# Attention scores as two fp32r passes over stacked key parts, the residual parked in HBM, and the attention half of the output projection woven in by tile

## The chip, the cores and the metric

The kernel runs on one core of a Trainium2 chip. A core has five engines that run beside each other and wait for one another by semaphores: TensorE (PE, matrix products and transposes; PEld is its weight load), VectorE (DVE), ScalarE (ACT), GpSimd (POOL) and SyncE (SP, which here only issues DMA transfers). Each engine works through its own list of instructions in order. The metric is the time of one execution on the device in microseconds (us), as the median of several runs.

## The reference, cut to what matters

One decoder layer on 512 rows of 1024 numbers, all in float32: a SwiGLU block, LN1, two mixers side by side on the same rows, LN2, a second SwiGLU block with an embedding, LN3.

```python
x = layer_norm(alpha * x + 0.5 * swiglu_ffn(x, ffn1_w13[i], ffn1_w2[i]), ln1_g[i], ln1_b[i])
h = x @ w_in[i]
...
y_a = gdn_mixer(gq, gk, gv, gz, ga, gb, ...)        # gated delta rule, 4 heads of 128
y_b = diff_attention_mixer(dq, dk, dv, ...)         # below
mix = jnp.concatenate([y_a, y_b], axis=-1)
x = layer_norm(alpha * x + mix @ w_out[i], ln2_g[i], ln2_b[i])
```

The change is in the attention, whose four heads hold two maps of 64 dimensions each; their scores are `q k^T` for each map, masked, through two softmaxes, and the second map is subtracted:

```python
s = jnp.einsum("bqhmd,bkhmd->bhmqk", qb, k).astype(f32) * scale      # d = 64, m = 0, 1
s = jnp.where(qp[:, None] >= pos[None, :], s, -jnp.inf)
pr = jax.nn.softmax(s, axis=-1)
attn = pr[:, :, 0] - lam * pr[:, :, 1]
return jnp.einsum("bhqk,bkhd->bqhd", attn.astype(v.dtype), v)
```

## The kernel before

The 512 rows are four tiles `t` of 128. A weight product in near-float32 precision is made of three products in fp32r, a reduced form of float32: each operand is split in a high part (a copy rounded to fp32r, on ACT) and a low part (the operand less its high part, on DVE), and `mm3` (lines 295 to 299) multiplies high by high, low by high and high by low. `split` (line 158) makes the parts. `XH`, `XL` hold the parts of the layer's rows, transposed; `RES` is the residual, four tiles of 128 x 1024 float32 that stay in the core's memory (SBUF).

The mixers (`mix_zone`) run in one zone of SBUF, with the residual beside it. First come straight parts: the values (`values_and_gates`), the keys and queries of the delta rule (`keys_queries`). LN1 of the four tiles is still under way when they begin: `norm_natural` of each tile takes statistics on DVE (L309), a power on POOL (L314), scales on DVE (L320, L329) and on ACT and POOL (L324, L325, L326), and `norm_turn` (L341) transposes it into `XH`, `XL`. The rest is written as generators, "lanes", that yield an estimated cost and wait; `weave` interleaves them by a running clock. The lanes are the delta rule's dense part (`gdn`), its block inverse (`diagonal`), its chain over four chunks (`chain`), sixteen `attention(t, h)` lanes, `fill` (attention keys and queries, other projections), and last `out_attn` and `out_gdn`, the two halves of the output projection with the residual addition and LN2. A scheduler below this settles the final list of each engine, and may set an instruction ahead of others that were written earlier.

In `fill`, the queries and keys of one tile are transposed and copied (L1003) to `DQT` and `DKT`. An attention lane makes, for each map `m`, one float32 product of 64 rows (the map's dimensions) into PSUM tag `c` (L1156) and adds the mask by a bf16 product of 128 rows (L1157). Then follow the maximum, the exponentials, a normalising combination (L1158 to L1165), the transposes (L1169), the product with the values `DV` (L1175) and an RMS norm that puts its output back over `DQT` (L1183). `TT`, a tile of 128 x 2048, holds the delta rule's inverse blocks; it is cleared at line 851 and later takes LN2's gains.

`out_attn` opens when all sixteen heads are done. It transposes and splits the attention's output of all four tiles (`to_mix`, PSUM tag `c`, L871), takes four weights, and then makes the 96 products of `project_out`, which lie between the steps of `chain`. These are the lines of the scores:

```python
for m in range(2):
    r = slice(m * DQK, (m + 1) * DQK)
    pe.matmul(sc[m], DQT[r, h, t * P:(t + 1) * P], DKT[r, h, 0:n], start=True, stop=False)
    pe.matmul(sc[m][:, n - P:n], idb, negb, start=False, stop=True)
    dve.tensor_reduce(mx[:, m:m + 1], sc[m], AX.X, ALU.max)
```

Here `n` is the number of keys that tile `t` may see, 128 x (t + 1).

## Time and profile before

| | |
|---|---|
| median of 3 runs | 1092.85 us (1091.51 to 1092.94) |
| the profiled execution | 1093.08 us, of which the span from first to last instruction is 1091.3 us |
| mean granted TensorE clock | 0.998 of full speed |
| TensorE products busy | 1067.6 us, 98% of the span |
| VectorE, ScalarE, GpSimd busy | 76%, 45%, 10% |
| mixers, from the values to LN2 | about 355 to 684 us of the span |

A busy TensorE in the records is not TensorE at its peak: products are pipelined and their records overlap. What a product costs is read from the distance between the starts of two neighbours in the timeline, and this distance is called its pitch here.

### The profile page before, as it was taken

The numbers are of one execution on the slowest core, as the hardware profiler recorded it, in microseconds if no ns is written. First come the engines' busy times: TensorE is split into PE (matmuls) and PEld (weight loads), VectorE is DVE, ScalarE is ACT, GpSimd is POOL, SyncE is SP. The second block draws the span as 40 slices with busy tenths as digits, with TensorE's granted clock in tenths as the row PEclk, the third lists the DMA queues.
The fourth block names the chain that finished last, engine by engine and source line by source line (L and its number), as shares of the span: only waits on it lengthen the run. The fifth ranks groups of instructions, "written<-read, shape, count | busy, mean of one in ns | idle before, by whom it ended". The sixth has DMA issues, their size and how long they took to land.

```text
span 1091.3 us, 17360 instructions
## 1 busy us (share of the span) xinstructions
PE 1067.6 (98%) x6627; PEld 941.4 (86%) x6627; DVE 826.3 (76%) x1446; ACT 491.3 (45%) x950; POOL 110.9 (10%) x175
## 2 busy tenths in 40 slices
PE   9999999999999989999999999999999999999996
PEld 7889898989897968778865887789899998999895
DVE  5989796979678366357674658889988796979568
ACT  5745352535333256324365633545444453535231
POOL 1100000000002302432112203100000000000003
PEclk9999999999999999999999999999999999999999
DMA  8634332333242042124120211524342332333212
GB/s 296 200 112 117 97 114 80 117 104 110 77 127 87 1 136 78 35 73 116 40 59 1 77 36 51 177 67 142 111 123 90 110 104 88 118 105 98 78 39 97
DMA packets 44275, 106.03 MB, mean 97 GB/s; under 512 B 10848, under 2 KB 12528, under 8 KB 44192
## 3 DMA queue, kind: packets, MB, share of 16 engines
q1 hardware_dynamic: 37968, 96.71, 29.1%
q0 software_dynamic: 1808, 6.04, 1.6%
q10 hardware_dynamic: 4416, 2.16, 0.7%
q8 instruction: 52, 0.85, 0.3%
q14 instruction: 31, 0.25, 0.1%
HBM read 102.41 MB, written 2.49 MB: 96 GB/s over the span
## 4 chain that ended last, share of the span: by engine, by line
PE 55%; DVE 5%; DMA 3%; ACT 2%; POOL 2%; issue 1%; DVEq 0%; SPq 0%; ACTq 0%; POOLq 0%
PE pb L297 9%; PE pb L298 9%; PE pb L299 9%; PE pc L299 4%; PE pc L298 4%; PE pc L297 4%; PE pa L299 3%; PE pa L298 3%; PE pa L297 3%; DMA raw<-in_wa_dram 3%; PE pc L1156 2%; DVE wl L160 1%; ACT wh L159 1%; PE pa L1089 1%; PE pc L1175 1%
## 5 line engine op out<-in xcount | busy, mean ns | idle before, releaser
L160 DVE TENSOR_TENSOR wl<-raw,wh 128x1024 fp32r<-128x1024 f32 (+3 forms) x137 | 142.2, 1044 | 42.0 <-ACT wh L159 40.9
L159 ACT CAST wh<-raw 128x1024 fp32r<-128x1024 f32 (+3 forms) x137 | 122.9, 905 | 104.3 <-PE pa L298 30.7
L297 PE MATMUL pb<-wh,hh 128*128 128x512 f32 (+1 forms) x356 | 138.3, 389 | 3.5 <-DVE RES L807 1.7
L298 PE MATMUL pb<-wl,hh 128*128 128x512 f32 (+1 forms) x356 | 138.0, 388 | 0.0
L299 PE MATMUL pb<-wh,hl 128*128 128x512 f32 (+1 forms) x356 | 137.8, 387 | 0.0
L229 ACT CAST th<-tr 128x512 fp32r<-128x512 f32 x160 | 98.5, 619 | 84.5 <-PE pc L298 49.6
L233 DVE TENSOR_TENSOR tl<-tr,th 128x512 fp32r<-128x512 f32 x160 | 109.1, 684 | 11.1 <-ACT th L229 10.2
L190 ACT CAST wh<-raw 128x512 fp32r<-128x512 f32 x88 | 54.4, 622 | 133.0 <-PE pb L299 91.4
L297 PE MATMUL pb<-wh,XH 128*128 128x512 f32 (+2 forms) x288 | 110.8, 385 | 3.1 <-ACT AB L928 1.3
L298 PE MATMUL pb<-wl,XH 128*128 128x512 f32 (+2 forms) x288 | 106.7, 371 | 1.2 <-DVE wl L160 1.1
L299 PE MATMUL pb<-wh,XL 128*128 128x512 f32 (+2 forms) x288 | 106.1, 368 | 0.0
L298 PE MATMUL pa<-XL,wh 128*128 128x256 f32 (+1 forms) x344 | 100.0, 291 | 0.3 <-DVE XL L160 0.3
L299 PE MATMUL pa<-XH,wl 128*128 128x256 f32 (+1 forms) x344 | 99.9, 290 | 0.0
L297 PE MATMUL pa<-XH,wh 128*128 128x256 f32 (+1 forms) x344 | 99.9, 290 | 0.0
L297 PE MATMUL pc<-XH,th 128*128 128x256 f32 x320 | 90.6, 283 | 0.0
L298 PE MATMUL pc<-XL,th 128*128 128x256 f32 x320 | 90.6, 283 | 0.0
L299 PE MATMUL pc<-XH,tl 128*128 128x256 f32 x320 | 90.6, 283 | 0.0
L490 DVE TENSOR_TENSOR RES<-RES,pb 128x512 f32<-128x512 f32 (+1 forms) x81 | 54.6, 677 | 45.3 <-PE pb L299 44.4
L191 DVE TENSOR_TENSOR wl<-raw,wh 128x512 fp32r<-128x512 f32 x88 | 60.0, 688 | 31.2 <-ACT wh L190 30.8
L297 PEld LDWEIGHTS pb<-wh,hh 128*128 128x128 f32 x356 | 66.9, 188 | 19.1 <-DVE RES L807 2.0
L299 PEld LDWEIGHTS pb<-wh,hl 128*128 128x128 f32 x356 | 66.9, 188 | 13.6
L298 PEld LDWEIGHTS pb<-wl,hh 128*128 128x128 f32 x356 | 66.9, 188 | 13.3 <-DVE wl L191 0.3
(303 smaller groups left out, 2639.1 us busy)
## 6 DMA issues: line engine op xcount, KB each, us to landing
raw<-in_wa_dram SPq DMA_DIRECT2D x127, 512.0 KB, 3.7
raw<-in_wb_dram SPq DMA_DIRECT2D x88, 256.0 KB, 2.7
raw<-in_wd_dram SPq DMA_DIRECT2D x4, 520.0 KB, 3.6
RES<-in_xn_dram POOLq DMA_DIRECT2D x4, 512.0 KB, 6.0
gb<-in_gb_dram POOLq DMA_DIRECT2D x8, 256.0 KB, 3.9
xr<-in_xT_dram ACTq DMA_DIRECT2D x7, 256.0 KB, 4.5
out_dram<-RES SPq DMA_DIRECT2D x5, 256.0 KB, 2.1
TT<-in_gb_dram POOLq DMA_DIRECT2D x4, 256.0 KB, 3.5
```

Of the source, the lines that this page charges most:

```text
L159: return (self.nc.scalar.copy(hi, src), self.nc.vector.tensor_tensor(lo, src, hi.bitcast(F32), ALU.subtract))
L160: self.nc.vector.tensor_tensor(lo, src, hi.bitcast(F32), ALU.subtract))
L190: nc.scalar.copy(hi, r)
L191: nc.vector.tensor_tensor(lo, r, hi.bitcast(F32), ALU.subtract)
L229: act.copy(h, t)
L233: dve.tensor_tensor(hl[1], t, hl[0].bitcast(F32), ALU.subtract)
L297: pe.matmul(o, wh, xh, start=first, stop=False)
L298: pe.matmul(o, wh, xl, start=False, stop=False)
L299: pe.matmul(o, wl, xh, start=False, stop=last)
L490: dve.tensor_tensor(rj, rj, pd, ALU.add)
L1089: pe.matmul(pt[:, h * P:(h + 1) * P], MP[:, 0, c, h, :], TT[:, c, h, :], start=True, stop=True)
L1156: pe.matmul(sc[m], DQT[r, h, t * P:(t + 1) * P], DKT[r, h, 0:n], start=True, stop=False)
```

## The change

1. **Scores.** For each map the 64 rows of keys become 128: `KK[:, m]` holds the keys' high parts on the map's own rows and their low parts on the other map's rows. `QZ` holds for each head and map the query's high part on both halves (`q = m`), and the query's low part on the map's rows over zeros (`q = 2 + m`). A score is two fp32r products of 128 rows. The parts are made by ACT copies and DVE subtractions: in `fill` for the keys, and at the start of each attention lane for the queries (a new yield follows them).
2. **Residual.** The four tiles of `RES` become one tile `RESA`. After LN1 all four are stored to `XR` in HBM. The first two then serve as `TT` (cleared in `keys_queries` now, not at the zone's start), the last two as `DQT`. They are loaded again from `XR` in `out_attn`.
3. **Output projection.** `out_attn` opens when the delta rule's dense part and the gate projection are done, and takes one tile at a time, when that tile's four heads are done; `to_mix` there uses PSUM tag `b`. LN2's gains lie in `DV`. `project_out` yields half its cost after every second weight.

```diff
-        self.RES = [cp.tile([P, D], F32, name=f"RES{t}") for t in range(NT)]
+        self.RESA = cp.tile([P, NT, D], F32, name="RESA")
+        self.RES = [self.RESA[:, t] for t in range(NT)]
...
-        TT = mp.tile([P, NC, H, P], F32, name="TT")
...
-        DKT = mp.tile([P, H, S], F32, name="DKT")
-        DQT = mp.tile([P, H, S], F32, name="DQT")
+        KK = mp.tile([P, 2, H, S], F32R, name="KK")
+        QZ = mp.tile([P, 4, 4, P], F32R, name="QZ")
+        DQT = [self.RESA[:, 2 + t // 2, (t % 2) * 512:(t % 2) * 512 + 512].rearrange("p (h b) -> p h b", b=P)
+               for t in range(NT)]
+        TT = self.RESA[:, 0:2].rearrange("p c (d h b) -> p (c d) h b", d=2, b=P)
...
-        pool.memset(TT, 0.0)
+        XR = dp.tile([NT, P, D], F32, name="XR")
...
                     held = (i, h)
+                    if i == 0 and h == 2:
+                        for t in range(NT):
+                            nc.sync.dma_start(XR[t], RES[t])
+                    if i == 1 and h == 0:
+                        pool.memset(TT, 0.0)
...
-                    dve.tensor_copy((DKT if word == "k" else DQT)[:, :, t * P:(t + 1) * P], v4(pt))
+                    if word == "k":
+                        for m in range(2):
+                            r, o = rows(m), rows(1 - m)
+                            hi = KK[r, m, :, t * P:(t + 1) * P]
+                            act.copy(hi, v4(pt)[r])
+                            dve.tensor_tensor(KK[o, m, :, t * P:(t + 1) * P], v4(pt)[r], hi.bitcast(F32), ALU.subtract)
+                    else:
+                        dve.tensor_copy(DQT[t], v4(pt))
...
             n = (t + 1) * P
+            i = (t * H + h) % 4
+            qz = QZ[:, i]
+            for m in range(2):
+                r, o = rows(m), rows(1 - m)
+                act.copy(qz[r, m], DQT[t][r, h])
+                act.copy(qz[o, m], DQT[t][r, h])
+                dve.tensor_tensor(qz[r, 2 + m], DQT[t][r, h], qz[r, m].bitcast(F32), ALU.subtract)
+            yield 0, 1.5
...
-                r = slice(m * DQK, (m + 1) * DQK)
-                pe.matmul(sc[m], DQT[r, h, t * P:(t + 1) * P], DKT[r, h, 0:n], start=True, stop=False)
+                for q in (m, 2 + m):
+                    pe.matmul(sc[m], qz[:, q], KK[:, m, h, 0:n], start=q == m, stop=False)
                 pe.matmul(sc[m][:, n - P:n], idb, negb, start=False, stop=True)
...
-            yield 0.2 + 0.43 * (t + 1), 4.5 + 0.8 * t
+            yield 0.1 + 0.24 * (t + 1), 4.5 + 0.8 * t
...
-                yield 2.6, 0
+                    if k % 2:
+                        yield 1.3, 0
...
+        done = [{("attn", t, h) for h in range(H)} for t in range(NT)]
+
         def out_attn():
-            for t in range(NT):
-                to_mix(DQT[:, :, t * P:(t + 1) * P], t, 4, "c")
-                yield 0.5, 0
+            for t in (0, 1):
+                nc.sync.dma_start(RES[t], XR[t])
             w = [self.take() for _ in range(4)]
             for t in range(NT):
+                while not done[t] <= said:
+                    yield 0, 0.5
+                to_mix(DQT[t], t, 4, "b")
+                if t % 2:
+                    nc.sync.dma_start(RES[2 + t // 2], XR[2 + t // 2])
+                yield 0.5, 1.0
                 yield from project_out(w, 0, t)
...
-            gbt = [TT[:, j].rearrange("p a b -> p (a b)") for j in range(4)]
+            gbt = [DV[:, j].rearrange("p a b -> p (a b)") for j in range(4)]
...
-        need_out = {("attn",) + th for th in heads} | {"z"}
+        need_out = {("gdn", c) for c in range(NC)} | {"z"}
```

Three places in the lists of the engines show what moved. The first is TensorE's list at the first two attention heads (tile 0, 128 keys, both maps). `pc` is the PSUM tile of the scores, `wh` and `XH` are parts of a weight product that lies between. Before:

```order
L1156 MATMUL pc_5135<-DKT,DQT 128x128
L1157 LDWEIGHTS idb
L1157 MATMUL pc_5135<-LVM,idb 128x128
L1156 MATMUL pc_5152<-DKT,DQT 128x128
L1157 LDWEIGHTS idb
L1157 MATMUL pc_5152<-LVM,idb 128x128
L297 MATMUL pb_5177<-wh_4720,XH 128x512
```

And now (the lines are shifted by the edit: L1156 is L1187, L1157 is L1188, L297 is L298):

```order
L1187 MATMUL pc_5180<-KK,QZ 128x128 x2
L1188 LDWEIGHTS idb
L1188 MATMUL pc_5180<-LVM,idb 128x128
L1187 MATMUL pc_5199<-KK,QZ 128x128 x2
L1188 LDWEIGHTS idb
L1188 MATMUL pc_5199<-LVM,idb 128x128
```

One float32 product of 64 rows has become two fp32r products of 128 rows, and the mask's product behind each pair has stayed.

The second place is POOL's list around LN1 of the last two tiles (t = 2 and t = 3), where `bnrs` holds a tile's statistics. Before, the clearing of `TT` stood behind the last tile:

```order
L325 TENSOR_TENSOR RES_70<-RES_70,gb_3794 128x256
L326 TENSOR_TENSOR RES_70<-RES_70,gb_3795 128x256
L314 TENSOR_TENSOR bnrs_3979<-bnrs_3979,mhalf 128x1
L316 TENSOR_SCALAR bnrs_3979<-bnmv_3977,bnrs_3979 128x1
L325 TENSOR_TENSOR RES_71<-RES_71,gb_3794 128x256
L326 TENSOR_TENSOR RES_71<-RES_71,gb_3795 128x256
L314 TENSOR_TENSOR bnrs_4037<-bnrs_4037,mhalf 128x1
L316 TENSOR_SCALAR bnrs_4037<-bnmv_4035,bnrs_4037 128x1
L325 TENSOR_TENSOR RES_72<-RES_72,gb_3794 128x256
L326 TENSOR_TENSOR RES_72<-RES_72,gb_3795 128x256
L851 MEMSET TT 128x2048
```

Now (L314 is L315, L316 is L317, L326 is L327) it stands between tile 1 and tile 2:

```order
L326 TENSOR_TENSOR RESA<-RESA,gb_3791 128x256
L327 TENSOR_TENSOR RESA<-RESA,gb_3792 128x256
L986 MEMSET RESA 128x2048
L315 TENSOR_TENSOR bnrs_3976<-bnrs_3976,mhalf 128x1
L317 TENSOR_SCALAR bnrs_3976<-bnmv_3974,bnrs_3976 128x1
L326 TENSOR_TENSOR RESA<-RESA,gb_3791 128x256
L327 TENSOR_TENSOR RESA<-RESA,gb_3792 128x256
L315 TENSOR_TENSOR bnrs_4034<-bnrs_4034,mhalf 128x1
L317 TENSOR_SCALAR bnrs_4034<-bnmv_4032,bnrs_4034 128x1
```

The clearing has moved ahead of six operations of LN1, and it now writes over the first two residual tiles, which the stores to `XR` read.

The third place is TensorE's list where the last tile of the attention enters the output projection. Before, the last of four transposes to `XH`, `XL` stood ahead of the products of tile 0, which read other columns:

```order
L871 MATMUL pc_6337<-CST,DQT 128x128 x4
L1202 MATMUL pa_6344<-ST_4066,KQ 128x128 x2
L1210 MATMUL pa_6354<-ST_4066,KQ 128x128 x4
L871 MATMUL pc_6363<-CST,DQT 128x128 x4
L297 MATMUL pb_6370<-wh_5957,XH 128x512
L298 MATMUL pb_6370<-wl_5958,XH 128x512
L299 MATMUL pb_6370<-wh_5957,XL 128x512
```

Now the transposes of tile 3 stand directly ahead of the products of tile 3 (L874 was L871):

```order
L299 MATMUL pb_6731<-wl_6203,XH 128x512
L300 MATMUL pb_6731<-wh_6202,XL 128x512
L874 MATMUL pb_6745<-CST,RESA 128x128 x4
L298 MATMUL pb_6753<-wh_5900,XH 128x512
L299 MATMUL pb_6753<-wl_5901,XH 128x512
L300 MATMUL pb_6753<-wh_5900,XL 128x512
```

The first product behind the transposes reads what ACT makes of them, and the third what DVE makes of that.

## Rows read from the trace of the kernel before

**Rows 1.** The profile's page: span, and busy time of TensorE.

```profile
span 1091.3 us, 17360 instructions
PE 1067.6 (98%) x6627; PEld 941.4 (86%) x6627; DVE 826.3 (76%) x1446; ACT 491.3 (45%) x950; POOL 110.9 (10%) x175
```

**Rows 2.** Windows view, attention's stretch: from:to, length, then busy us of each engine.

```profile
480.00:611.00 131.00, 129.41 (x723) 97.83 (x722) 85.55 (x226) 69.75 (x158) 24.94 (x54) 1.00 0.17 50
```

**Rows 3.** Timeline of PE, two score runs: start us, duration us, instruction.

```profile
489.03 0.27 PE L1169 MATMUL pc<-CST,tt 128*128 128x128 f32 x1
489.23 0.48 PE L1156 MATMUL pc<-DKT,DQT 64*128 64x128 f32 x2
...
490.00 0.40 PE L298 MATMUL pb<-wl,XH 128*128 128x512 f32 x1
...
577.34 0.49 PE L1169 MATMUL pc<-CST,tt 128*128 128x128 f32 x3
577.75 1.12 PE L1156 MATMUL pc<-DKT,DQT 64*128 64x512 f32 x2
578.81 0.23 PE L1157 MATMUL pc<-LVM,idb 128*128 128x128 bf16 x1
578.85 0.48 PE L298 MATMUL pb<-wl,XH 128*128 128x512 f32 x1
579.16 0.40 PE L299 MATMUL pb<-wh,XL 128*128 128x512 f32 x1
```

**Rows 4.** Timeline of PE, fp32r products of 256 and of 512 columns.

```profile
360.56 0.28 PE L297 MATMUL pb<-wh,XH 128*128 128x256 f32 x1
360.68 0.28 PE L298 MATMUL pb<-wl,XH 128*128 128x256 f32 x1
...
498.00 0.40 PE L297 MATMUL pb<-XH,wh 128*128 128x512 f32 x1
498.24 0.39 PE L298 MATMUL pb<-XL,wh 128*128 128x512 f32 x1
```

**Rows 5.** Source view of line 1156: count, duration ns min/median/max, first and last start, forms.

```profile
L1156 PE MATMUL pc<-DKT,DQT x64: 272/481/693, 480.4 to 599.3; 64*128 64x128 f32 x16, 64*128 64x256 f32 x16, 64*128 64x384 f32 x16, 64*128 64x512 f32 x16
```

**Rows 6.** Groups by line and form, ACT and DVE, 380 to 612: busy us, mean ns.

```profile
L1171 ACT COPY tt<-pc 128x128 f32<-128x128 f32 x4 | 1.0, 262 | 2.0 <-PE pc L1169 2.0
L1165 DVE SCALAR_TENSOR_TENSOR tt<-pc,arr,tt 128x128 f32<-128x128 f32 x4 | 1.4, 346 | 0.0
```

**Rows 7.** Timelines of POOL, DVE, ACT and PE at LN1; brackets: idle before, releaser.

```profile
352.07 0.73 POOL L326 TENSOR_TENSOR RES<-RES,gb 128x256 f32<-128x256 f32 x1
354.60 0.99 POOL L314 TENSOR_TENSOR bnrs<-bnrs,mhalf 128x1 f32<-128x1 f32 x1 [1.80 <-DVE bnrs L313]
357.30 0.67 DVE L490 TENSOR_TENSOR RES<-RES,pb 128x512 f32<-128x512 f32 x1
363.89 1.81 POOL L851 MEMSET TT<- 128x2048 f32 x1
363.87 0.37 ACT L926 COPY DV<-pb 128x256 f32<-128x256 f32 x1 [1.02 <-POOL RES L326]
364.36 0.39 PE L297 MATMUL pb<-wh,XH 128*128 128x264 f32 x1 [1.27 <-ACT AB L928]
```

**Rows 8.** The page's DMA issues: queue, count, KB each, median us from issue to landing.

```profile
raw<-in_wa_dram SPq DMA_DIRECT2D x127, 512.0 KB, 3.7
out_dram<-RES SPq DMA_DIRECT2D x5, 256.0 KB, 2.1
```

**Rows 9.** Timeline of PE, the chain's last transposes to XH, XL and what follows.

```profile
658.15 1.02 PE L871 MATMUL pa<-CST,ta 128*128 128x128 f32 x4 [0.21 <-DVE ta L1249]
659.44 0.50 PE L297 MATMUL pb<-wh,XH 128*128 128x512 f32 x1 [0.27 <-DVE RES L1274]
```

**Rows 10.** Timeline of PE, last Gram product of the delta rule, first product with the inverse.

```profile
471.29 1.46 PE L1071 MATMUL pa<-KQ 128*128 128x256 f32 x6
503.47 0.60 PE L1089 MATMUL pa<-TT,MP 128*128 128x128 f32 x4
```

More of the change, by code (lines that the diff above doesn't have):

```diff
@@ L993, in keys_queries, with rows @@
                 pool.tensor_tensor(NRM[:, c], q1[:, c], phalf[:, 0:H], ALU.pow)
+        def rows(m):
+            return slice(m * DQK, (m + 1) * DQK)
         def fill():
@@ L1011, in fill @@
                             turn(*held)
+                    if word == "q" and t == 0:
+                        for m in range(2):
+                            pool.memset(QZ[rows(1 - m), :, 2 + m].bitcast(F32), 0.0)
                     d = tb()
@@ L1145, in attention @@
             n = (t + 1) * P
+            i = (t * H + h) % 4
+            qz = QZ[:, i]
+            for m in range(2):
+                r, o = rows(m), rows(1 - m)
[3 more added lines that the diff above has]
+            yield 0, 1.5
             if t < 2:
@@ L1175, in attention @@
                 pe.matmul(po[:, 0:P], at[:, c * P:(c + 1) * P], DV[:, c, h, :], start=c == 0, stop=c == t)
-            y = DQT[:, h, t * P:(t + 1) * P]
+            y = DQT[t][:, h]
             so = stat([P, 4], "aso")
```

## Prediction

> **What bounds the kernel now.** I read the page first: TensorE is busy for 1067.6 of 1091.3 us, and no other engine comes near [rows 1]. The windows view says whether that holds where the change is made. In the attention's 131 us TensorE is busy for 129.4, VectorE for 85.6, ScalarE for 69.8 [rows 2]. So in the mixers time is won by taking work off TensorE's list, and lost where TensorE is made to wait. The timelines of PE give the price of a piece of that list, by the distance between starts. The other engines' timelines at LN1 give the one place where the change puts a new wait into a chain that TensorE already waits for.
>
> **Scores, before.** A transpose of 128 columns has a pitch of 0.11: one lasts 0.27 and three lasted 0.49, so two more added 0.22. In the run with 128 keys the transpose at 489.03 gives way at 489.14, and the second product behind the scores starts at 490.00 [rows 3]. Between them lie the score pair, its mask and one weight product, whose pitch is 0.23 (498.00 to 498.24) [rows 4]. The pair with its mask costs 490.00 - 489.14 - 0.23 = 0.63 us. With 512 keys: three transposes from 577.34 end at 577.67, the second product behind starts at 579.16, so 1.26 us [rows 3]. There are sixteen records of each of the four widths [rows 5], which is eight pairs (a float32 product leaves two records). Taken as even steps, 256 and 384 keys cost 0.84 and 1.05. The sum is 8 x (0.63 + 0.84 + 1.05 + 1.26) = 30.2 us.
>
> **Scores, after.** An fp32r product of 128 rows has a pitch of 0.12 with 256 columns and 0.23 with 512 [rows 4]; 384 lie between, at 0.175. No fp32r product with 128 columns is in the trace. I take 0.11, as for the transposes of that width. The mask stays: 0.04 to the next start (578.81 to 578.85), and that next product holds the engine for 0.31 instead of 0.23, so 0.12 in all [rows 3]. A pair is now two passes and a mask: 8 x (2 x (0.11 + 0.12 + 0.175 + 0.23) + 4 x 0.12) = 14.0 us. The gain is 30.2 - 14.0 = **16.2 us**. Bounds: if the 0.08 behind the mask belongs to the 64-row product ahead of it and goes, 32 x 0.08 = 2.6 more; if 128 columns cost half of 256, 16 x 0.05 = 0.8 more. If each 128-column pass costs as much as a 64-row record (0.48 - 0.27 = 0.21), 16 x 0.10 = 1.6 less; if the 0.09 ahead of a pair (489.14 to 489.23) stays too, 32 x 0.09 = 2.9 less. So 11.7 to 19.6.
>
> The row shows about 0.2 us a pair that is neither record [rows 3]. The Trainium skill, TensorEngine Tiling (Array Packing), section Key Properties, says that a change of tiling mode, unlike a change of tile, drains TensorE. By that rule all of this overhead comes from the 64-row products, the 0.08 goes as well, and the gain would be 18.8 instead of 16.2. I stay with the smaller, since the mask is also a change of number format, which stays.
>
> **The parts of queries and keys.** Each of 16 heads adds four ACT copies and two DVE subtractions of 64 rows x 128; priced as 128 x 128 rows (0.26 and 0.35), that is 64 x 0.26 = 16.8 us on ACT and 32 x 0.35 = 11.1 on DVE [rows 6]. The four key tiles add eight copies and eight subtractions of 512 columns, at most four times such a row each: 8.4 and 11.1. Put into the attention's stretch whole, DVE comes to 107.8 and ACT to 95.0 of about 115 us [rows 2]. That is no bound by sums, and I cost it at nothing. Its cover is that DQT is long finished when a head's turn comes, and weight products of `fill` and of the projection stand ahead of the scores. Without that cover it is a rival, below.
>
> **The clearing of TT.** It now overwrites the residual tiles that the stores to XR read, and stands on POOL ahead of tile 2's power. Tile 1's last residual operation ended at 352.07 + 0.73 = 352.80 [rows 7]. Only then can its store be issued. I price the store by the load of the same size, 3.7 us to landing; the 256 KB store, 2.1, is the lower end [rows 8]. The clearing takes 1.81, so tile 2's power, which started at 354.60, starts at 352.80 + 3.7 + 1.81 = 358.3, **3.7 us** later (2.1 at the lower end). Behind it on POOL lie both tiles' remaining LN1 steps; behind tile 2's scaling on DVE lies L490 (357.30), which frees a PSUM bank. TensorE feels it: the copies of the values at 363.87 waited for POOL, and TensorE waited 1.27 us for them at 364.36 [rows 7]. It had no slack there, so all 3.7 count. [...]
>
> **The projection of tile 3.** Before, the four `to_mix` lay among the chain's products, with tile 0's work behind them. Now the transposes of tile 3 stand directly ahead of products that read them. The nearest case starts its transposes at 658.15 and the next product at 659.44 [rows 9]; 0.44 of these 1.29 are the transposes, so TensorE stands for 0.85. With DVE's half needed at the third product I take **1.2 us** (0.85 to 1.5). The restoring load of the last residual tile is issued there too: some 0.5 + 3.7 us after the transposes begin, while its first use comes after twelve products, 0.44 + 1.2 + 12 x 0.23 = 4.4. It is just covered. The weight loads queued behind it on SP need their buffers freed by the same products anyway. The other restores and the four stores go through an idle queue, at nothing.
>
> **The block inverse.** From the end of the last Gram product (471.29 + 1.46 = 472.75) to the first product with the inverse (503.47) TensorE had 30.7 us of other work [rows 10]. Adding up the new list between the same two by the pitches above leaves 27.3. How much of the 30.7 the inverse needs, the rows don't say: 0 to 3.4. I take **1.0**.
>
> **Sum**, against the profiled execution's 1093.1 (0.2 above the median): 1093.1 - 16.2 + 3.7 + 1.2 + 1.0 = 1082.8, hence 1082.6 as a median.
>
> **Rivals.**
> A. *The clearing is hidden.* If the store lands soon or TensorE finds other products, 3.7 falls away: 1078.9, and 1076.3 with the larger score gain. For it: the DMA engines are idle there. Against it: the list leaves POOL no way around.
> B. *The passes are dear.* The lead-in and a slow 128-column pass keep the gain at 11.7: 1087.1, and 1089.5 with the inverse's full 3.4. For it: no row shows such a pass. Against it: the 256-column pitch is half that of 512.
> C. *Every head's scores wait for its parts* (the other side). Four copies and a subtraction in a row take 4 x 0.26 + 0.35 = 1.4 us, behind whatever ACT has queued. If TensorE has nothing else then, 16 x 1.4 = 22.4 us come on top: 1105. It decides from 12.2 / 16 = 0.76 us a head, where the time passes 1095. For it: ACT and DVE get fuller while TensorE's cover shrinks by a tenth. Against it: the copies need only DQT, which is ready early.
> D. *The change gives nothing back.* Faster mixers reach the second SwiGLU block earlier, and its weights, issued in order on SP, don't come earlier: the 16.2 turn into waits there, about 1092. For it: TensorE has little to do but weight products there. Against it: loads are issued when buffers come free, and the same products free them.
>
> **Chances.** The forecast (1080 to 1086) 0.50, A 0.17, B 0.14, C 0.12, D 0.07. For this kernel 0.2%, or 2.2 us, is about what can be told from no change. C is mostly slower, with a part at half its price inside or below the 2.2; D is mostly no change. So faster 0.81, same 0.09, slower 0.10. The range takes A's and B's ends and stops short of D and C: 1076 to 1091.
>
> **What would show it.** Right: TensorE's records for the score line with 128 rows, at a pitch of 0.11 to 0.23, and its busy time in the attention some 16 us less; POOL's clearing starting about 3.7 us after the first store-ready moment, tile 2's power behind it, and TensorE's wait at the last values product grown from 1.3 to about 5 us; a wait of about 1 us behind the transposes of tile 3. Wrong: waits of TensorE on the QZ copies in front of score after score (C), score passes with a pitch of 0.2 at 128 columns (B), a clearing that starts at once (A), or a wait for weights at the start of the second SwiGLU block (D).

## The result, and the profile after

The changed kernel takes 1100.09 us as a median of 4 runs (1098.41 to 1100.80), the kernel before 1092.89 beside it (1091.51 to 1095.24). The ratio is 1.0068, interval 1.0051 to 1.0085: about 7 us slower, where 10 us faster was forecast. The profiled executions differ by 7.7 us of span. On the page, TensorE's busy time fell and its share with it, where before it was 1067.6 and 98% [rows 1]; ACT and DVE grew, and two rows are new, the stores and loads of the residual:

```profile
span 1099.0 us, 17503 instructions
...
PE 1060.6 (97%) x6627; PEld 945.1 (86%) x6627; DVE 838.5 (76%) x1482; ACT 513.6 (47%) x1021; POOL 109.7 (10%) x177
...
XR<-RESA SPq DMA_DIRECT2D x4, 512.0 KB, 2.6
RESA<-XR SPq DMA_DIRECT2D x4, 512.0 KB, 3.3
```

TensorE has less to do and is later. The view of waits, for PE from 340 to 700 us (total us, times, longest us), says what it stood for. All its rows add up to 21.7 us, against 8.4 before:

```profile
PE pb L298 <- ACT tb L1034: 2.3, 1, 2.3
PE pa L1258 <- ACT ta L1250: 2.3, 1, 2.3
PE pc L1187 <- DVE amx L1189: 2.0, 1, 2.0
PE pb L298 <- ACT AB L931: 1.9, 1, 1.9
PE pc L1200 <- DVE tt L1196: 1.7, 1, 1.7
PE pa L1248 <- DVE VV L1235: 1.7, 2, 1.1
PE pb L298 <- DVE RESA L491: 1.6, 1, 1.6
```

The two rows with RESA and AB are LN1 and the values, where the clearing works. The rows with `tb` L1034 and `amx` are single waits at 477 and 490 us, ahead of the first heads' scores and between them. The rows with `tt` and `ta` L1250 lie from 594 to 601 us, at the end of `fill`. The windows view (us, PE, PEld, DVE, ACT and POOL busy, then the granted clock as a share of full speed, DMA share, GB/s) shows a second loss at the last three places. Its first row answers to [rows 2], where TensorE was busy for 129.41 us at full clock:

```profile
480.00:611.00 131.00, 122.11 (x719) 104.29 (x719) 85.98 (x235) 82.18 (x209) 22.85 (x49) 0.95 0.21 62
...
480.00:482.00 2.00, 2.00 (x5) 1.61 (x6) 0.00 (x0) 0.00 (x0) 1.49 (x5) 0.50 0.23 66
476.00:484.00 8.00, 5.70 (x19) 4.24 (x19) 3.53 (x13) 1.75 (x3) 2.89 (x6) 0.79 0.22 33
488.00:498.00 10.00, 8.00 (x36) 6.31 (x36) 8.24 (x39) 6.02 (x22) 1.84 (x6) 0.83 0.09 28
598.00:606.00 8.00, 5.72 (x27) 5.50 (x28) 2.98 (x7) 6.13 (x19) 2.46 (x3) 0.57 0.27 88
```

Behind the waits at these three places the clock falls (behind the two of LN1, 1.6 and 1.9 us, it stays at 1.00); from 480 to 482 it is 0.50, the lower of its two levels, 1.2 instead of 2.4 GHz. Before, the same stretches had 1.00. Not granted are 8 x 0.21 + 10 x 0.17 + 8 x 0.43 = 6.8 us of full speed (part of it while TensorE stood anyway). So 13.3 us of new waits and up to 6.8 of slower products came on top, and a net loss of 7.7 means that the list itself got shorter by 5.6 to 12.4, by this estimate.

The timeline of PE (start, duration, instruction, idle before and its releaser) shows the passes and the two early waits:

```profile
479.79 0.80 PE L298 MATMUL pb<-wh,XH 128*128 128x512 f32 x1 [2.30 <-ACT tb L1034]
480.38 0.63 PE L299 MATMUL pb<-wl,XH 128*128 128x512 f32 x1
480.81 0.63 PE L300 MATMUL pb<-wh,XL 128*128 128x512 f32 x1
...
489.19 0.39 PE L300 MATMUL pb<-wh,XL 128*128 128x512 f32 x1
489.41 0.33 PE L1187 MATMUL pc<-KK,QZ 128*128 128x128 f32 x2
489.59 0.23 PE L1188 MATMUL pc<-LVM,idb 128*128 128x128 bf16 x1
489.63 0.42 PE L1187 MATMUL pc<-KK,QZ 128*128 128x128 f32 x2
489.88 0.23 PE L1188 MATMUL pc<-LVM,idb 128*128 128x128 bf16 x1
492.11 0.44 PE L1187 MATMUL pc<-KK,QZ 128*128 128x128 f32 x2 [2.00 <-DVE amx L1189]
...
609.88 0.71 PE L1187 MATMUL pc<-KK,QZ 128*128 128x512 f32 x2
610.43 0.23 PE L1188 MATMUL pc<-LVM,idb 128*128 128x128 bf16 x1
610.47 0.71 PE L1187 MATMUL pc<-KK,QZ 128*128 128x512 f32 x2
```

With 128 keys a pair and its mask take 0.22 us (489.41 to 489.63) where a weight product stands ahead, and 0.29 behind another mask (489.63 to 489.88, and 0.04 for the mask). With 512 keys they take 0.59 (609.88 to 610.47). The pitch of a weight product is 0.43 (480.38 to 480.81) where the clock is low, against 0.23 before [rows 4]. What TensorE waited for stands in ACT's timeline:

```profile
476.14 0.58 ACT L1018 CAST KK<-pb 64x512 fp32r<-64x512 f32 x1 [4.53 <-PE pb L874]
476.61 1.89 ACTq L1136 DMA_DIRECT2D blocks<-MP  x4
478.55 0.58 ACT L1018 CAST KK<-pb 64x512 fp32r<-64x512 f32 x1 [1.83 <-issue]
479.15 0.59 ACT L1034 COPY tb<-pb 128x512 f32<-128x512 f32 x1
...
486.89 0.30 ACT L1173 CAST QZ<-RESA 64x128 fp32r<-64x128 f32 x1 [7.15 <-DVE RESA L1021]
...
593.58 1.28 ACT L1192 ACT_TABLE_LOAD   x1
...
596.00 1.04 ACT L160 CAST wh<-raw 128x1024 fp32r<-128x1024 f32 x1
...
598.37 1.28 ACT L1063 ACT_TABLE_LOAD   x1
...
600.16 0.58 ACT L1250 COPY ta<-pa 128x512 f32<-128x512 f32 x1
```

At 476 the second of two key copies is queued behind four DMA issues that hold ACT for 1.89 us. Behind it stands L1034, whose copy frees one of the two PSUM buffers of tag `b`, and TensorE needs that for its next weight product. At 487 to 492 sixteen QZ copies run in a burst, for four heads at once; they begin as soon as DVE has copied tile 0's queries to `DQT` (L1021). DVE's timeline shows what this does to the maximum of the first scores (L1189), which TensorE waits for until 492.11:

```profile
491.08 0.32 DVE L1175 TENSOR_TENSOR QZ<-RESA,QZ 64x128 fp32r<-64x128 f32 x1
...
491.78 0.28 DVE L1189 TENSOR_REDUCE amx<-pc 128x1 f32<-128x128 f32 x1
```

The scores are there at 490.1, but their maximum stands in DVE's list behind steps of the block inverse and two subtractions for the next heads (490.38 and 491.08), which read what ACT copies. At 593 to 600 ACT has the exponentials, the next weights' high parts, two table loads and the chain's copy `ta` one behind the other, and TensorE waits for the last.

### The profile page after: what moved, and what is told of

Read it like the earlier page. It is cut to its first block, busy times and chain, and to the rows that moved or that the text cites. A ratio compares the mean times of both kernels' runs of the same rounds, so it can differ in the third digit from the quotient of the medians.

```text
span 1099.0 us, 17503 instructions
## 1 busy us (share of the span) xinstructions
PE 1060.6 (97%) x6627; PEld 945.1 (86%) x6627; DVE 838.5 (76%) x1482; ACT 513.6 (47%) x1021; POOL 109.7 (10%) x177
## 4 chain that ended last, share of the span: by engine, by line
PE 51%; DVE 6%; ACT 4%; DMA 3%; POOL 2%; issue 2%; ACTq 0%; DVEq 0%; POOLq 0%
PE pb L298 9%; PE pb L299 9%; PE pb L300 8%; PE pc L299 4%; PE pc L298 4%; PE pc L300 4%; PE pa L299 3%; PE pa L300 3%; PE pa L298 3%; DMA raw<-in_wa_dram 2%; DVE wl L161 2%; ACT wh L160 1%; PE pc L1187 1%; PE pa L1110 1%; PE pa L874 1%
## 5 line engine op out<-in xcount | busy, mean ns | idle before, releaser
L298 PE MATMUL pb<-wh,hh 128*128 128x512 f32 (+1 forms) x356 | 138.5, 390 | 4.6 <-DVE RESA L808 1.7
L300 PE MATMUL pb<-wh,hl 128*128 128x512 f32 (+1 forms) x356 | 137.8, 387 | 0.0
L298 PE MATMUL pb<-wh,XH 128*128 128x512 f32 (+2 forms) x288 | 111.1, 386 | 8.1 <-ACT tb L1034 2.3
L300 PE MATMUL pb<-wh,XL 128*128 128x512 f32 (+2 forms) x288 | 107.4, 373 | 0.0
L298 PE MATMUL pa<-XH,wh 128*128 128x256 f32 (+1 forms) x344 | 100.0, 291 | 0.0
L300 PE MATMUL pa<-XH,wl 128*128 128x256 f32 (+1 forms) x344 | 99.9, 290 | 0.0
L298 PE MATMUL pc<-XH,th 128*128 128x256 f32 x320 | 90.6, 283 | 0.0
L300 PE MATMUL pc<-XH,tl 128*128 128x256 f32 x320 | 90.6, 283 | 0.0
L491 DVE TENSOR_TENSOR RESA<-RESA,pb 128x512 f32<-128x512 f32 (+1 forms) x81 | 54.6, 677 | 45.2 <-PE pb L300 44.3
L298 PEld LDWEIGHTS pb<-wh,hh 128*128 128x128 f32 x356 | 66.9, 188 | 20.2 <-DVE RESA L735 2.1
L300 PEld LDWEIGHTS pb<-wh,hl 128*128 128x128 f32 x356 | 66.9, 188 | 13.8
```

Of the source, the lines that this page charges most:

```text
L298: pe.matmul(o, wh, xh, start=first, stop=False)
L300: pe.matmul(o, wl, xh, start=False, stop=last)
L491: dve.tensor_tensor(rj, rj, pd, ALU.add)
```

## The experiments

Each ratio is against runs of the kernel before on the same chip. The theory to begin with: the parts on ACT and DVE cost TensorE its cover at the first heads, and the clearing costs what was forecast. The rivals: the passes are dear, the projection by tile is at fault, or the order is.

**The clearing moved behind LN1.** POOL clears the two tiles by multiplying ones with zero, written in `gates_decay`.

```diff
+            for c in range(NC):
+                pool.tensor_scalar(TT[:, c], bc(ones, 1, H), 0.0, None, ALU.mult)
...
-                    if i == 1 and h == 0:
-                        pool.memset(TT, 0.0)
```

> The clearing of TT is written as four multiplications by zero of a tile that POOL fills behind LN1, so it stands behind LN1 of all tiles on POOL. Theory (the clearing delays LN1 and TensorE has no slack there): tile 2's power starts near 355 again instead of 358.5, TensorE's marks behind LN1 come about 2.5 us earlier, time about 1097.6. Rival (what LN1 loses is made good later by waits that shrink): the marks move at LN1, but the time stays at 1100 within 1.

Measured: 1094.81 against 1092.02, ratio 1.0033 (1.0021 to 1.0044). Two timelines of POOL show it, first after, then this kernel:

```profile
356.76 1.81 POOL L986 MEMSET RESA<- 128x2048 f32 x1 [3.62 <-DMA XR<-RESA]
358.53 0.55 POOL L315 TENSOR_TENSOR bnrs<-bnrs,mhalf 128x1 f32<-128x1 f32 x1
```

```profile
353.90 0.99 POOL L315 TENSOR_TENSOR bnrs<-bnrs,mhalf 128x1 f32<-128x1 f32 x1 [1.80 <-DVE bnrs L314]
```

The clearing stood for 3.62 us until the store had landed, and tile 2's power moved from 354.60 [rows 7] to 358.53; here it is at 353.90 again. TensorE begins its last Gram products 3.8 us sooner than in after (474.64 there, 470.84 here), of which 1.0 lies ahead of LN1's first transposes (347.38 against 348.40), before the two kernels differ: the clearing cost it 2.8, near the 2.5 expected, and the time fell by more than expected. A loss of 0.33% stays, with the same waits of 2.3, 2.0, 1.7 and 2.3 us.

**Parts of the queries made for tile 0 alone** (tiles 1 to 3 use those of tile 0; the clearing as in after).

```diff
-            for m in range(2):
+            for m in range(2 if t == 0 else 0):
```

> Only the first four heads make their query parts; the other twelve multiply with the parts of the first tile, so the output is another one. 48 ACT copies of 0.30 us and 24 DVE subtractions of 0.28 us are left out. Theory (ACT and DVE queues with the parts in them make TensorE wait): the waits between 586 and 606 (about 6.6 us, and some 2.5 us of lower clock behind them) shrink by more than half; time 1094 to 1096. The waits at 477 and 490, which the first four heads and the key parts cause, stay. Rival (the weave of attention, chain and projection makes these waits, whatever ACT does): under 1.5 us, 1099 to 1100.

Measured: 1095.93 against 1092.02, 1.0036 (1.0023 to 1.0049). The later parts cost some 0.3% as well. The time is the one that the theory gave, but its waits shrink by a third and not by more than half: those listed from 586 to 606 fall from 5.9 to 4.0 us, and the clock from 575 to 615 rises from 0.91 to 0.96. The wait for `ta` at `fill`'s end stays, 2.7 us: it isn't made by the query parts of tiles 1 to 3.

**The projection's attention half at the end again** (part 3 undone; parts 1 and 2 stay).

```diff
-                    if k % 2:
-                        yield 1.3, 0
+                yield 2.6, 0
...
+            for t in range(NT):
+                to_mix(DQT[t], t, 4, "c")
...
             w = [self.take() for _ in range(4)]
             for t in range(NT):
-                while not done[t] <= said:
-                    yield 0, 0.5
-                to_mix(DQT[t], t, 4, "b")
...
-        need_out = {("gdn", c) for c in range(NC)} | {"z"}
+        need_out = {("attn",) + th for th in heads} | {"z"}
```

> The third part of the change alone is undone: out_attn opens when all heads are done, transposes all four tiles through tag c and yields once per eight rows of work, as before. Theory (ACT's queue makes the waits; the projection's weight splits are now on ACT among the last heads): fewer splits among the heads, so some of the waits at 586 to 606 go, time 1096 to 1099. Rival (the order by tile is what costs): all of them go, 1091 to 1095. Second rival (the projection's products are the cover of the late heads): TensorE waits more, 1102 to 1106.

Measured: 1107.28, 1.0143 (1.0128 to 1.0158), against 1.0068 with it. It is no culprit but cover, as the second rival had it: without its products the waits grow, as in the waits of PE from 590 to 660:

```profile
PE pc L1200 <- DVE tt L1196: 4.1, 2, 2.4
PE pa L1258 <- ACT ta L1250: 2.6, 2, 2.3
```

**The scores undone** (part 1 undone; the clearing and the projection stay).

```diff
-                        for m in range(2):
-                            ...
+                        dve.tensor_copy(KK[:, 0, :, t * P:(t + 1) * P], v4(pt))
...
-            yield 0, 1.5
...
-                for q in (m, 2 + m):
-                    pe.matmul(sc[m], qz[:, q], KK[:, m, h, 0:n], start=q == m, stop=False)
+                r = rows(m)
+                pe.matmul(sc[m], DQT[t][r, h], KK[r, 0, h, 0:n], start=True, stop=False)
```

> The first part alone is undone: float32 scores of 64 rows, no parts of keys or queries; residual in HBM and projection by tile stay. Theory (the score gain of 16 us on TensorE's list is real and the parts give back part of it): the list grows by 16, the waits at 477 and 490 with their low clock (8 us) and part of those at 586 to 606 go: 1102 to 1106. Rival (the two passes gain little, the parts cost much): 1092 to 1097.

Measured: 1098.51, 1.0060 (1.0045 to 1.0075), between the expectations. Its waits add up to 10.7 and none is longer than 2.1; from 575 to 615, at the end of `fill`, none is longer than 0.6. So the two-pass scores with all that hangs on them are worth nothing in after (1.0068 against 1.0060, no difference beyond the intervals), and parts 2 and 3 together lose the 0.6% by themselves.

**No parts at all** (with the late clearing; keys by one DVE copy, QZ only cleared: the scores are those of zeros, the instructions of TensorE stay).

```diff
-            for m in range(2):
-                r, o = rows(m), rows(1 - m)
-                act.copy(qz[r, m], DQT[t][r, h])
-                act.copy(qz[o, m], DQT[t][r, h])
-                dve.tensor_tensor(qz[r, 2 + m], DQT[t][r, h], qz[r, m].bitcast(F32), ALU.subtract)
...
+                        dve.tensor_copy(KK[:, 0, :, t * P:(t + 1) * P], v4(pt))
```

> On top of the late clearing (measured 1094.8): no parts are made at all. The keys get one DVE copy per tile as before the change, used for both maps, and the query tile is only cleared; the scores are therefore others, while every product, mask and softmax stays. Theory (the parts on ACT and DVE are what the gain is paid back with): the waits of 2.5 and 2.2 us in front of the first scores and most of those at 582 to 595, with the lower clock behind each, go; time 1080 to 1085. Rival (the order of chain, attention and projection makes TensorE wait at 582 to 640): only the first two waits go, 1086 to 1090.

Measured: 1085.71 against 1091.25, 0.9954 (0.9938 to 0.9970). Against the first experiment (1.0033) that is 0.79%: the parts, with the waits for them, cost 8.6 us, give or take 2 by the two intervals. The windows of this kernel:

```profile
468.00:500.00 32.00, 31.92 (x161) 26.50 (x160) 17.16 (x60) 9.43 (x25) 11.09 (x27) 1.00 0.33 80
584.00:596.00 12.00, 8.22 (x39) 7.71 (x40) 6.25 (x17) 7.67 (x22) 3.62 (x5) 0.72 0.32 108
```

At the first heads TensorE is busy throughout and at full clock. At the end of `fill` it still stands, in PE's timeline for a head and for the chain:

```profile
585.02 0.52 PE L1190 MATMUL pc<-CST,tt 128*128 128x128 f32 x3 [1.08 <-DVE tt L1186]
588.29 2.08 PE L1248 MATMUL pa<-ta,KD 128*128 128x128 f32 x8 [2.76 <-ACT ta L1240]
```

Four kernels, all with the late clearing and so to be held against 1.0033, tried to make the parts without the waits. **The DMA issues of the inverse's blocks off ACT:**

```diff
-                (nc.scalar if b % 2 else nc.sync).dma_start(
+                nc.sync.dma_start(
```

> On top of the late clearing: the four DMA issues of the block inverse's first step that ACT makes (1.89 us on its queue) go to SP. Theory (the 2.5 us wait of TensorE before the first scores is ACT's queue: two key copies of 0.58 and these issues stand ahead of the copy that frees the PSUM bank): the wait shrinks to about 0.6 or less and the low clock behind it (about 1.6 us) goes; time about 1091, 3 to 4 less. Rival (the bank is freed late by DVE's key subtraction, or the lost time comes back at the inverse): under 1 us.

Measured: 1096.44, 1.0045 (1.0029 to 1.0061). The wait for `tb` fell from 2.30 to 1.22, so these issues were about half of it. But the inverse came later (first product at 514.16, in the first experiment at 505.57) and two new waits of 1.10 and 0.98 us appeared at 500 and 505: nothing is gained, as the rival had it. **Half of the copies on POOL:**

```diff
-                act.copy(qz[o, m], DQT[t][r, h])
+                pool.tensor_copy(qz[o, m], DQT[t][r, h])
```

> On top of the late clearing: the second of each two query copies (32 of 0.30 us on ACT) goes to POOL. Theory (ACT's queue makes the waits): ACT gets 9.6 us shorter; the wait of 2.2 us at the first heads and part of those at 582 to 595 shrink; time 1090 to 1093. Rival (POOL's own queue, where the copy stands behind rotary and norm steps that wait, delays the scores more): 1095 to 1100.

Measured: 1095.71, 1.0047 (1.0029 to 1.0064). The wait between the heads went from 2.0 to 1.5, the one for `tb` stayed at 2.3, and a new one of 1.2 came; nothing is gained. **Parts once for a tile**, four copies and two subtractions of 64 x 512 instead of sixteen and eight, and a yield at the tile's first head only:

```diff
+            if h == 0:
+                while t > 0 and ("score", t - 1, H - 1) not in said:
+                    yield 0, 0.3
...
+                    act.copy(QZ[r, :, m], DQT[t][r])
+                    act.copy(QZ[o, :, m], DQT[t][r])
+                    dve.tensor_tensor(QZ[r, :, 2 + m], DQT[t][r], QZ[r, :, m].bitcast(F32), ALU.subtract)
```

> On top of the late clearing: the query parts are made once per tile for its four heads (4 copies and 2 subtractions of 64 x 512 in place of 16 and 8 of 64 x 128), and only the first head of a tile yields for them. In TensorE's list the first score of tile 3 then stands at row 3155 instead of 3194. Theory (the parts load ACT and push the heads back in the order): the wait of 2.2 us at the first heads goes, those at 582 to 595 shrink; time 1088 to 1091. Rival (the 4 x 0.6 us of copies in front of each tile's first head cost as much as the small ones): 1093 to 1096.

Measured: 1092.16 against 1091.24, 1.0010 (0.9999 to 1.0022), between the expectations: the only one of the four that helps. The wait between the heads fell from 2.0 to 0.8, the one for `tb` stayed at 2.3, the one for `ta` L1250 is gone. **The new yield left out:**

```diff
-            yield 0, 1.5
```

> On top of the late clearing: the yield of 1.5 us behind a head's parts is taken out and nothing else; the parts stay, sixteen times four copies. The heads stand earlier in TensorE's list (first score of tile 3 at row 3134 instead of 3194, last of tile 3 at 3211 instead of 3260). Theory (part of the loss is the order: the yield holds two heads in flight 1.5 us longer each, so the heads of tiles 2 and 3 fall behind the fill that would cover them): the waits at 582 to 640 shrink, those in front of the first scores grow; time 1089 to 1093. Rival (ACT's load alone): the scores wait for their parts one by one, 1096 to 1101.

Measured: 1098.19, 1.0064 (1.0047 to 1.0081). The yield that puts other work between a head's parts and its scores is worth 0.3%. That the scores then wait one by one isn't shown: TensorE waits for QZ for 0.5 us in all, and longest, 3.2 and 2.2 us, for the inputs `tb` of transposes at 565 and 507.

What is left lies at the end of `fill`. **Three heads at a time** instead of two, on top of the parts by tile, should cover one head's exponentials with another's:

```diff
-            if i >= 2:
-                need.add(("attn",) + heads[i - 2])
+            if i >= 3:
+                need.add(("attn",) + heads[i - 3])
```

> The kernel with parts per tile, and three heads in flight instead of two in the planner's rule (first score of tile 3 at row 3084, last at 3160, both earlier than before the change). Theory (attention as a chain of latencies has lost its cover): the heads run under the fill as before the change, the waits at 582 to 640 go, time 1082 to 1087. Rival (PSUM tag c and ACT cannot hold three heads): TensorE waits for banks in front of the scores, 1092 to 1098.

Measured: 1091.13, 1.0002 (0.9992 to 1.0013), between the expectations again. The end of `fill` is filled in this kernel, as the same stretch shows, first before the change, then here:

```profile
575.00:615.00 40.00, 38.93 (x200) 27.23 (x200) 21.41 (x49) 26.78 (x62) 11.13 (x16) 1.00 0.13 42
575.00:615.00 40.00, 38.86 (x226) 32.08 (x225) 19.97 (x49) 24.60 (x55) 13.35 (x18) 1.00 0.25 80
```

In after TensorE was busy for 34.07 us of it, at a clock of 0.91. What was won there went to other places: the waits from 340 to 700 add up to 14.4 us, against 8.4 before. **The same without parts** (on the kernel without parts):

> The kernel without any parts (1085.7; its scores are others, see there) with three heads in flight instead of two in the planner's rule; the first score of tile 3 stands at row 3121 of TensorE's list instead of 3193. Theory (what the kernel without parts still loses is the order: heads so late that the fill no longer covers them, and chain and heads share ACT): the waits at 583 to 592 and their low clock (about 7 us) go; time 1078 to 1081, where the prediction's sum without the clearing stands. Rival (that loss is not the order): 1085 to 1088.

Measured: 1092.84 against 1091.38, 1.0013 (1.0002 to 1.0024), slower than two heads without parts (0.9954). ACT's timeline of this kernel:

```profile
599.70 1.04 ACT L160 CAST wh<-raw 128x1024 fp32r<-128x1024 f32 x1 [2.40 <-PE pb L300]
600.76 1.28 ACT L1182 ACT_TABLE_LOAD   x1
602.06 0.69 ACT L1182 ACTIVATE tt<-pc,amx 128x512 f32<-128x512 f32 x1
```

Here TensorE stands for 4.5 us at once. The split of the next weights waits for one of its products (L300) to free a buffer, and on ACT the exponentials stand behind that split and a table load. The theory that more heads fill this place fell for this kernel. A rival is left: from 470 to 620 it loads ACT's tables (1.28 us each) fifteen times, the kernel without parts and with two heads twelve times, the one with parts and three heads eleven times; no run separates these loads from the order. **The keys' high parts on DVE**, on top of three heads:

```diff
-                            act.copy(hi, v4(pt)[r])
+                            dve.tensor_copy(hi, v4(pt)[r])
```

> The kernel with three heads and parts per tile (1091.1), with the high parts of the keys copied by DVE instead of ACT. Theory (TensorE's wait of 2.3 us before the first scores is the copy of the next query tile, which stands on ACT behind the keys' second part and the block inverse's DMA issues): the wait falls below 0.6, time 1087 to 1089, below both kernels. Rival (the wait only moves, as it did when the DMA issues were moved, since DVE now frees the bank late): 1090 to 1092.

Measured: 1091.43 against 1091.38, 0.9996 (0.9981 to 1.0011). The longest wait only changes its engine, in the waits of PE from 340 to 700:

```profile
PE pb L298 <- DVE KK L1019: 2.0, 1, 2.0
```

Two last kernels separate the scores' new costs in the planner from their place beside `fill`. **The old costs and no yield, without parts:**

```diff
-            yield 0, 1.5
...
-            yield 0.1 + 0.24 * (t + 1), 4.5 + 0.8 * t
+            yield 0.2 + 0.43 * (t + 1), 4.5 + 0.8 * t
```

> The kernel without parts (1085.7; its scores are others, see there), with the planner's numbers for the heads put back: no yield of 1.5 us behind the parts, and the old costs of the scores. The heads then stand in TensorE's list nearly where they stood before the change (first scores of the four tiles at rows 2798, 2903, 3019, 3135, against 2798, 2903, 3007, 3113 before and 2807, 2964, 3076, 3193 without this). Theory (what remains lost without parts is the place of the heads against the fill): the waits at 583 to 592 go, 1077 to 1081. Rival (cover: the heads' chain of ACT and DVE steps has lost TensorE work to hide behind wherever it stands, above all at the end of the fill, where the next four weights must first be split): the waits appear elsewhere, 1084 to 1089.

Measured: 1097.67 against 1091.53, 1.0058 (1.0039 to 1.0077). Its windows view:

```profile
600.00:614.00 14.00, 9.17 (x47) 8.11 (x47) 6.11 (x16) 9.82 (x21) 3.77 (x6) 0.63 0.25 80
```

TensorE stands for 4.8 of 14 us at the end of `fill`, at a clock of 0.63: without parts, the hole stays with two heads, with three, and in the old order. The fourth experiment has the same costs, no yield and no parts either; it differs by the long scores and the early clearing. The same stretch in both, first the fourth, then this one:

```profile
575.00:615.00 40.00, 38.93 (x198) 27.27 (x197) 21.20 (x47) 27.01 (x58) 11.19 (x17) 1.00 0.12 38
575.00:615.00 40.00, 33.03 (x171) 26.40 (x170) 21.06 (x49) 26.90 (x61) 10.13 (x17) 0.87 0.19 58
```

With the long products TensorE is busy there, with the short ones it stands. Two things changed along with them: the scheduler placed some other products elsewhere, and ACT loads its tables sixteen times from 470 to 620 instead of thirteen. **The old costs, with parts by tile:**

```diff
-            yield 0.1 + 0.24 * (t + 1), 4.5 + 0.8 * t
+            yield 0.2 + 0.43 * (t + 1), 4.5 + 0.8 * t
```

> The kernel with parts per tile (two heads in flight, 1092.2 or 1.001 of before), with the old costs of the scores in the planner. The first scores of tiles 1 to 3 stand 4 to 12 rows earlier. Theory of the order: 1088 to 1090. Rival of cover: 1091 to 1093, no difference.

Measured: 1093.30 against 1091.53, 1.0013 (1.0003 to 1.0024), as with the new costs (1.0010).

## Why the prediction was wrong

- **Where the difference lies.** Parts 2 and 3 of the change were forecast at 3.7 + 1.2 us and cost 0.60% or 6.6 us (the fourth experiment). Part 1 was forecast at a gain of 16.2 less 1.0 for the inverse and is worth nothing in after. So nearly all of the 17 us that are missing lie in part 1.
- **The step that failed** is the one on the parts of queries and keys: "That is no bound by sums, and I cost it at nothing." The sizes were right: in the groups of after, the copies and subtractions have 32 x 0.30 us twice and 8 x 0.58 on ACT, 32 x 0.29 and 8 x 0.69 on DVE, 23.6 and 14.7 us together against 25.2 and 22.2 allowed. The busy sums were right too. Queue order was not looked at. Of the first key copies one stands ahead of L1034 and behind four DMA issues on ACT, and the first sixteen QZ copies come as a burst. The cover that was named, "DQT is long finished when a head's turn comes", was not there for tile 0: its first copy began when DQT was written (486.89). Without parts, the time falls by 8.6 us (the fifth experiment against the first): this is shown.
- **Rival C** named this mechanism with the wrong shape: not 0.76 us or more at each of sixteen heads, but two waits of 2.3 and 2.0 us at the first heads, small ones later, and the products behind them at 0.79 and 0.83 of the clock.
- **No term for lost cover.** TensorE's shorter list was counted as time won everywhere. At the end of `fill`, by this account, the products that went had covered a head's exponentials, the split of weights and the chain's copy. Without any parts 1.1 and 2.8 us of waits stand there, with a clock of 0.72: that is some 4 to 7 us back, an estimate. The pair of the fourth and the thirteenth experiment points the same way, but the table loads and the order changed with the scores, so that the products alone do it isn't shown. Nor must it be so: with parts by tile and three heads the place is filled, and other waits have come for it. The Trainium skill, TensorE: Matmul & The Clock Gate, Part 1: The HAM clock gate, says that TensorE's clock has two states and that activity is what holds it up. The trace agrees: 0.50 at 480 to 482, behind a wait, by itself some 1.0 us.
- **Scores:** the mechanism was right, and the list got shorter by somewhat less than forecast. A pair with mask, and with what the mask adds to the next product, costs 0.29 us at 128 keys and 0.59 at 512, where 0.34 and 0.58 were worked out; before, 0.63 and 1.26. At 128 keys the first pair takes 0.18 to its mask and the second, behind a mask, 0.25: what a mask adds to the next product stays at 0.07, while the 0.09 ahead of a pair is gone (489.19 to 489.41 is a weight product's own 0.22). By the Trainium skill's rule on changes of tiling mode (TensorEngine Tiling (Array Packing), Key Properties) both would have gone with the 64-row products; the trace agrees on the second alone. The balance of the fifth experiment (5.3 us of span won, 5.4 of waits more than before, and up to 3.4 of clock, part of it while TensorE stood) gives a list shorter by 10.7 to 14.1, against 16.2. TensorE's busy time agrees: 1057.2 us, 10.4 less than before, with the slower products in it. The 2 to 6 us between are not assigned.
- **Clearing:** 3.7 forecast, with all of it on TensorE. Tile 2's power comes 3.9 us later, of which 2.8 reach TensorE (the first experiment). Undoing it gains 0.35% in all, 3.8 us; the rest may be clock, which is low in two stretches there and not in three. That this total comes so near 3.7 is luck: the wait at the last values product grew from 1.27 to 1.92 and not to 5, and another of 1.62 stands ahead, where products wait for L491.
- **Projection of tile 3:** 1.2 forecast, 1.0 found: the transposes at 652.20 and the next product at 653.47, with 0.67 of idle time, then 0.17 ahead of the third product. That it also serves as cover, worth 0.75% (the third experiment against after), was not seen.
- **Block inverse:** 1.0 forecast for the inverse itself. From the end of the last Gram product to it (474.64 + 1.02 = 475.66 to 510.87) after has 35.2 us, against 30.7 [rows 10]; without parts it is 29.2, and TensorE waits there for 0.4 in all, not for the inverse. So the term was 0 there; of the 4.5 more in after, 4.3 are the two waits at 477 and 490, which go with the parts.
- **Rival D** was not seen: at its first weights the second SwiGLU block waits 0.17 and 0.77 us at 715, against 0.18 and 0.76 at 707 before.
- **Open:** whether weights split earlier would cover the end of `fill`. The kernel has four weight buffers, and no run has more. With parts by tile and three heads the kernel just equals the one before (1.0002): TensorE's busy time is 9.1 us less than before (1058.5), and 6.0 us of this come back as waits. No version that makes its parts was faster than the kernel before beyond the interval.

## What to carry to other kernels

Price preparing work not by an engine's busy sum but by its place in that engine's queue: name the instruction that ends up behind it, and who waits for that one. When the engine that bounds a kernel gets less to do, ask too at which places its old work was the cover for somebody else's latency, and count these places as waits. Where memory gets a second use, look up where its clearing lands in the engine's list, since it now waits for the first use to end.

## What was not expected of the hardware

- A single wait of 2.0 to 2.3 us was followed by the low clock in after, with weight products at a pitch of 0.43 instead of 0.23. In the first experiment the same wait of 2.3 us, from 473.7 to 476.0, was not, while the one of 2.0 between the heads was; in the kernel with parts by tile the wait of 2.3 us was not either (1.00 from 472 to 486). The windows of the first experiment:

```profile
472.00:482.00 10.00, 7.70 (x37) 6.09 (x36) 5.05 (x17) 2.15 (x5) 2.92 (x6) 1.00 0.19 26
484.00:492.00 8.00, 6.00 (x28) 4.68 (x27) 6.61 (x35) 4.80 (x18) 1.86 (x6) 0.79 0.10 34
```

What sets the two apart these runs don't show.
- Four DMA issues on ACT's queue held up its next copy for 1.89 us (476.61 to 478.55). They stood there before as well, for 1.88 us from 473.70, and TensorE did not wait at all from 470 to 500: it had other products until the copy behind was done.
- The store of 512 KB lands after 2.6 us, a load of the same size after 3.3 to 3.7 [rows 8].
